# A hybrid mixer with a mixture of experts: the merge gates in three fp32r passes, attention's mask fused with its maximum, memory loaded first

## The chip, the cores and the metric

One core of a Trainium2 chip runs the whole kernel. The metric is the device time of one execution in microseconds (us); the input arrays lie in the chip's memory when it starts. The core's engines are TensorE (PE in the profile; its weight loads PEld), VectorE (DVE), ScalarE (ACT), GpSimd (POOL) and SyncE (SP), whose queue issues the transfers. The kernel before takes 1305.42 us, the median of 3 runs (1305.41 to 1307.28).

## The reference

Input x is 256 tokens of width 1024, fp32. One layer is computed:

```python
h = _layer_norm(x, ln_emb_g, ln_emb_b)
z = h @ w_in                      # split into q, k, v (three kinds), nsa gates, u, qm, g_mrg
y_nsa = _nsa(q, kc, vc, ks, vs, kw, vw, g_nsa, ...) @ w_nsa_out
y = _s5(u, ...)                   # a linear recurrence over the tokens, 32 groups x 64 states
ga, gb = split(gelu(y) @ w_s5_glu); y_s5 = ga * sigmoid(gb)
y_mem = _memory_attention(qm, mem, w_mem_kv) @ w_mem_out
g = sigmoid(g_mrg).reshape(B_, L, N_BRANCH, D_MODEL)
merged = g[:, :, 0] * y_nsa + g[:, :, 1] * y_s5 + g[:, :, 2] * y_mem
h = _layer_norm(ALPHA * h + merged @ w_o, ln1_g, ln1_b)
h = _layer_norm(ALPHA * h + _moe(h, ...), ln2_g, ln2_b)
```

The attention (`_nsa`) has 8 heads of 64 in 2 groups and three branches: over 15 compressed blocks, over selected blocks and over a window. Here all 256 tokens fall into both the selection and the window, each with a causal mask. The memory attention has 4 heads of 128 over 256 memory rows. The merge gates g_mrg are three products of h with a weight of 1024 x 1024 each, one for each branch. The experts are 32, each with weights of 1024 x 2048 and 1024 x 1024; a token goes to four of them.

## The kernel before

The kernel has three stages. The mixer (to some 345 us of the span) computes the layer norm of the input, all projections, the S5 branch, both attentions, the gates and the projection w_o. The router and the second layer norm follow. Then the 32 experts run one after another, and the last layer norm ends the kernel.

All weights come in chunks of 128 x 2048 fp32 (1 MB), each into one slot of four pools of slots (u, w, s, z with 11, 3, 4 and 4 slots). A transfer starts when its slot is free. Weights of the first experts are loaded ahead into slots of these pools as far as they are free. The queue of SyncE issues all these transfers in one fixed order.

The mixer's order of work is a string of steps, ORDER (line 49), which is written out by hand: v and k are memory values and keys, P0 to P7 the pairs of the S5 branch, V, q, r, m projections and rotations, c0 and c1 the two compressions, e0 and e1 the additions to h (the layer norm's scale and bias for the residual), a0 to a3, b0 to b3 and g0 to g3 the gates of the S5, the memory and the attention branch, N0 to N3 pairs of attention heads, h0 to h3 memory heads, s and o output products. Within an engine the framework's scheduler then orders the instructions of these steps, with this string as their priority, and the result is fixed when the program is built: an engine takes its instructions in that order and waits at the first whose data isn't there.

What the change touches:

A gate step (gate_step, line 710, through feature_major, line 230) loads one chunk of w_g, multiplies its 2 x 8 blocks of 128 x 128 with hT (the normalised input, features on partitions, 256 tokens) in fp32, and copies the 128 x 512 result out on ScalarE (line 712). In the profile each fp32 matmul has two records (`L238 ... mm<-hT,w`).

The output products (s, o, N's w_nsa_out, w_o) use another form: split (line 184) rounds a tile to fp32r on ScalarE (L186) and takes the rest by a subtraction on VectorE (L187), split_half (line 189) does so for half a chunk in a slot of pool s (tile hl), and mm3 (line 197) makes three fp32r matmuls (L199, L200, L201) from high and low parts.

An S5 pair (line 449) makes an angle tile on ScalarE (L456), rounds it by adding and subtracting a large number on VectorE (L457), subtracts (L458, in the profile by the helper's line L80) and goes on to sine and cosine, eight products (`v<-sc,z`, `z<-sc,z`), a scan (L485) and more products. The compressions c0 and c1 (line 576) transpose keys or values (L583), add a position vector on VectorE (`xa<-tr,s_pe_k_cmp`, by L80) and multiply (L597).

Attention (nsa_pair, line 659): for each of two token tiles t and two groups g the scores of two heads lie in a PSUM bank; VectorE adds the mask (`pr<-sc,mask`, by L80), takes the negated maximum (L679), ScalarE takes Exp with its sum (L681), VectorE inverts the sum, multiplies by the branch gate (L683, L684, L80) and scales the probabilities (L687), and TensorE transposes them (L696).

The loads at the start are issued in the order x, a small vector, mem, two chunks of w_memk, the first of w_u.

## Time and profile before

| | |
|---|---|
| runs | 1305.42 us median (1305.41 to 1307.28) |
| profiled execution | 1305.18 us, its span 1303.4 us |
| mean granted TensorE clock | 0.984 |
| TensorE busy | 1226.3 us (94%), 7085 records |
| VectorE busy | 578.5 us (44%) |
| ScalarE busy | 245.5 us (19%) |
| moved by the transfers | 451.94 MB, mean 347 GB/s |

The profile shows one execution. A row of a timeline gives when a group of like instructions starts, how long it lasts, its engine, line, operation and tiles, how many there are, and in brackets how long the engine stood idle before it and what ended the wait. Matmuls overlap: of a matmul the time from one start to the next counts, not its own length. A granted clock of 1.00 is 2.4 GHz, one of 0.50 is 1.2 GHz.

### The profile page before, as it was taken

How to read it: one execution, taken by the hardware profiler on the slowest of the kernel's cores; microseconds unless marked ns; L12 is line 12 of the kernel's file. 1: busy time of each engine (PE TensorE's matmuls, PEld its weight loads, DVE VectorE, ACT ScalarE, POOL GpSimd, SP SyncE). 2: the span in 40 equal slices, each digit the busy share in tenths (PEclk: the TensorE clock that was granted, in tenths of full speed). 3: DMA queues.
4: the chain of work that ended last, by engine and by line, in shares of the span. 5: the costliest groups of instructions: out<-in, count | busy, mean ns of one | idle time of the engine just before them, and what ended most of it. 6: DMA issues, size and time to landing. Idle time of an engine off the chain costs nothing. (4 is left out here: it accounts for less than half of the span.)

```text
span 1303.4 us, 17567 instructions
## 1 busy us (share of the span) xinstructions
PE 1226.3 (94%) x7085; PEld 608.4 (47%) x7086; DVE 578.5 (44%) x1337; ACT 245.5 (19%) x493; POOL 72.2 (6%) x138
## 2 busy tenths in 40 slices
PE   6998999999889999999999999999999999999994
PEld 5656887789644444333333334333333333333331
DVE  5598637488663223433333334333333433332225
ACT  4243315574301000110100011010000110100011
POOL 1000000000110000000000001000000100000001
PEclk9999899999889999999999999999999999999998
DMA  7334435445879999999999999999999999999992
GB/s 267 107 125 159 143 117 177 163 162 214 346 313 411 426 426 426 426 426 426 426 427 425 426 427 427 427 425 427 426 426 427 426 426 426 427 426 426 427 425 83
DMA packets 65333, 451.94 MB, mean 347 GB/s; under 512 B 8896, under 2 KB 9056, under 8 KB 11360
## 3 DMA queue, kind: packets, MB, share of 16 engines
q1 hardware_dynamic: 64960, 450.26, 84.1%
q8 instruction: 57, 0.93, 0.3%
q10 hardware_dynamic: 288, 0.52, 0.1%
q14 instruction: 28, 0.23, 0.0%
HBM read 449.70 MB, written 1.05 MB: 346 GB/s over the span
## 5 line engine op out<-in xcount | busy, mean ns | idle before, releaser
L1025 PE MATMUL pg<-w,xT 128*64 128x512 f32 x1024 | 266.0, 597 | 0.0
L1025 PE MATMUL pl<-w,xT 128*64 128x512 f32 x1024 | 262.7, 592 | 0.0
L1061 PE MATMUL py<-w,aT 128*64 128x512 f32 x1024 | 228.7, 599 | 0.0
L1043 DVE TENSOR_SCALAR gc<-pg 128x256 f32<-128x256 f32 x64 | 24.2, 419 | 336.7 <-PE pg L1025 336.7
L1025 PEld LDWEIGHTS pl<-w,xT 128*64 128x64 f32 x1024 | 78.7, 137 | 133.6 <-issue 125.7
L1068 DVE SCALAR_TENSOR_TENSOR ys<-py,gs,ys 128x512 fp32r<-128x512 f32 x64 | 48.0, 751 | 208.7 <-ACT ys L1067 205.3
L1061 PEld LDWEIGHTS py<-w,aT 128*64 128x64 f32 x1024 | 71.0, 137 | 132.5 <-issue 126.4
L1025 PEld LDWEIGHTS pg<-w,xT 128*64 128x64 f32 x1024 | 72.0, 136 | 129.5 <-issue 118.0
L238 PE MATMUL mm<-hT,w 128*128 128x256 f32 x512 | 120.0, 388 | 1.0 <-ACT hT L323 0.7
L1044 ACT ACTIVATE sg<-gc 128x256 f32<-128x256 f32 x64 | 23.1, 408 | 477.1 <-DVE gc L1043 477.1
L80 DVE TENSOR_TENSOR h<-h,pc 128x512 f32<-128x512 f32 x128 | 82.5, 682 | 56.9 <-PE pc L1076 55.2
L238 PEld LDWEIGHTS mm<-hT,w 128*128 128x128 f32 x512 | 96.3, 193 | 19.4 <-issue 4.9
L83 POOL TENSOR_TENSOR xT<-xT,lc 128x256 f32<-128x256 f32 x64 | 44.7, 698 | 785.0 <-PE py L1057 777.6
L1076 PE MATMUL pc<-ys,ohT 128*128 128x512 f32 x256 | 85.5, 435 | 0.9 <-DVE h L80 0.8
L1067 ACT ACTIVATE ys<-py,gs 128x512 fp32r<-128x512 f32 x64 | 44.0, 688 | 193.6 <-PE py L1061 193.6
L1076 PEld LDWEIGHTS pc<-ys,ohT 128*128 128x128 f32 x256 | 40.2, 188 | 65.8 <-issue 35.1
L1003 PE MATMUL xg<-oh,hb 128*128 128x64 bf16 x1280 | 51.6, 195 | 0.9 <-DVE oh L993 0.9
L1003 PEld LDWEIGHTS <-hb 128*128 128x128 bf16 x1280 | 47.9, 99 | 9.3 <-issue 8.2
L1051 ACT ACTIVATE aT<-pt 128x256 f32<-128x256 f32 x64 | 24.6, 384 | 120.1 <-PE pt L1050 120.1
L1003 PE MATMUL xg<-oh,bias 128*128 128x64 bf16 x256 | 46.1, 195 | 0.0
L1057 PE MATMUL py<-bias,sel 128*64 128x512 bf16 x64 | 25.6, 403 | 20.9 <-DVE lin L1047 20.9
L1050 PE MATMUL pt<-ident,gc 128*128 128x128 f32 x128 | 31.9, 330 | 12.7 <-ACT aT L1051 10.0
(387 smaller groups left out, 1288.4 us busy)
## 6 DMA issues: line engine op xcount, KB each, us to landing
w<-in_w_gate_up SPq DMA_DIRECT2D x256, 1024.0 KB, 19.6
w<-in_w_down SPq DMA_DIRECT2D x128, 1024.0 KB, 19.6
w<-in_w_g SPq DMA_DIRECT2D x12, 1024.0 KB, 5.2
w<-in_w_s_glu SPq DMA_DIRECT2D x4, 1024.0 KB, 4.7
w<-in_w_o SPq DMA_DIRECT2D x4, 1024.0 KB, 6.3
w<-in_w_memk SPq DMA_DIRECT2D x2, 1024.0 KB, 10.0
w<-in_w_u SPq DMA_DIRECT2D x2, 1024.0 KB, 8.9
w<-in_w_memv SPq DMA_DIRECT2D x2, 1024.0 KB, 5.2
```

The source lines that it names most:

```text
L80: V.tensor_tensor(o, x, y, op=op)
L83: G.tensor_tensor(o, x, y, op=op)
L238: PE.matmul(p[:, m * T:(m + 1) * T], w4[:, m, k, :], xT[:, k, :], start=k == 0, stop=k == KT - 1)
L1003: PE.matmul(xg[:, k, :], hb[t][b][:, (4 * i + k) * 128:(4 * i + k + 1) * 128], oh[:, t, :], start=n == 0, stop=n == 5)
L1025: PE.matmul(p_[hf * 64:(hf + 1) * 64, :], lhsT, w[:, o + hf * 512:o + (hf + 1) * 512], start=start, stop=stop)
L1050: PE.transpose(pt[:, c * 128:(c + 1) * 128], g2[:, i, :, c % 2], ident)
L1051: S.activation(aT[:, sl], pt[:, sl], AF.Copy)
L1057: PE.matmul(py[0:64, :], sel, bias[:, 2 * DFF + hf * 512:2 * DFF + (hf + 1) * 512], start=True, stop=False)
L1061: PE.matmul(py[j * 64:(j + 1) * 64, :], a4[:, k // 4, k % 4 + j, :], dn(k + j, hf), start=k + j == 1, stop=k == 6)
L1067: S.activation(y2[:, 0], py, AF.Copy, scale=gs)
L1068: V.scalar_tensor_tensor(y2[:, 1], py, gs, y2[:, 0].bitcast(F32), op0=OP.mult, op1=OP.subtract)
L1076: PE.matmul(pc, ohT[:, t * 128:(t + 1) * 128], ys[hf][:, i], start=i == 0, stop=i == 1)
```

## The change

Gates: hT is split once into hTh and hTl, each half of a chunk of w_g is split as for the output products, and 48 fp32r matmuls take the place of 16 in fp32. Order: c0 and c1 come behind a0 and a1 in place of ahead of e1, P7 comes ahead of b0. Attention: mask addition and maximum become one VectorE operation per head (tensor_tensor_reduce, with the maximum as its accumulator), the small operations serve four heads at once, and the scaling of the probabilities goes to ScalarE, in the memory heads too. S5: ScalarE makes the rounding's first half, VectorE the rest in one operation; two operations of the gelu go to ScalarE. Loads: mem and the first chunk of w_memk come ahead of x.

```diff
@@ -46,7 +46,7 @@
 
 NU, NW, NS, NZ = 11, 3, 4, 4
 PATTERN = "uuzzsuuuuwuwwuszssu"
-ORDER = ("v0 P0 v1 k0 P1 k1 P2 V0 P3 V1 q0 q1 r0 e0 r1 P4 P5 m0 c0 m1 c1 e1 a0 a1 P6 a2 a3 b0 b1 P7 "
+ORDER = ("v0 P0 v1 k0 P1 k1 P2 V0 P3 V1 q0 q1 r0 e0 r1 P4 P5 m0 m1 e1 a0 c0 a1 P6 c1 a2 a3 P7 b0 b1 "
          "Y C b2 b3 N0 g0 N1 h0 h1 g1 g2 L1 B g3 N2 h2 s0 s1 h3 L1 L1 N3 s2 s3 o0 o1")
 LOAD1, LOAD2, LOAD3 = 1, 1, 0
 WOT = "uzsssuzu"
@@ -267,10 +267,11 @@
             return emit
 
 
+        mem = load_rows("mem")
+        memk = [chunk(a["w_memk"][0])]
         xin = load_rows("x")
         lec = small("ln_emb_gc", [128, 2, KT])
-        mem = load_rows("mem")
-        memk = [chunk(a["w_memk"][c]) for c in range(2)]
+        memk.append(chunk(a["w_memk"][1]))
         w_u = [chunk(a["w_u"][0])]
         pos_i = small("positions", [128, NT], I32)
         lr = small("s5_a_re", [128, 16])
@@ -444,6 +445,8 @@
 
         half_pi = fp.tile([128, 1], F32)
         G.memset(half_pi, math.pi / 2)
+        magic = fp.tile([128, 1], F32)
+        G.memset(magic, MAGIC)
         ybank = [None]
 
         def s5_pair(jp):
@@ -453,9 +456,10 @@
             cw, sw, w0, w1 = (z4[:, i] for i in range(4))
             vr, vi, ph, sn = (v4[:, i] for i in range(4))
             for jj in range(2):
-                S.activation(ph[:, jj, :], tio, AF.Copy, scale=psh[:, 2 * jp + jj:2 * jp + jj + 1])
-            V.tensor_scalar(sn, ph, MAGIC, MAGIC, op0=OP.add, op1=OP.subtract)
-            tt(ph, sn, ph, OP.subtract)
+                sc_ = psh[:, 2 * jp + jj:2 * jp + jj + 1]
+                S.activation(ph[:, jj, :], tio, AF.Copy, scale=sc_)
+                S.activation(sn[:, jj, :], tio, AF.Identity, scale=sc_, bias=magic)
+            V.scalar_tensor_tensor(ph, sn, MAGIC, ph, op0=OP.subtract, op1=OP.subtract)
             for jj in range(2):
                 j = 2 * jp + jj
                 V.scalar_tensor_tensor(ph[:, jj, :], tio, psl[:, j:j + 1], ph[:, jj, :], op0=OP.mult, op1=OP.add)
@@ -555,7 +559,7 @@
                 S.activation(pm[:, t, :], s3[:, t, :], AF.Exp, bias=mx[:, t:t + 1], accum_out=sums[:, t:t + 1])
             V.reciprocal(sums, sums)
             for t in range(NT):
-                V.tensor_scalar(pm[:, t, :], pm[:, t, :], sums[:, t:t + 1], None, op0=OP.mult)
+                S.activation(pm[:, t, :], pm[:, t, :], AF.Copy, scale=sums[:, t:t + 1])
             p = bank("tr")
             for kk in range(2):
                 for t in range(NT):
@@ -668,23 +672,28 @@
                     PE.matmul(s3, qT[g * 64:(g + 1) * 64, i, t * 128:(t + 1) * 128],
                               kT[g * 64:(g + 1) * 64, :, 0:nk], start=True, stop=True)
                     scs.append(s3)
+
+                mx = f2.tile([128, 4], F32, tag="mx4", name="mx")
+                sums = f2.tile([128, 4], F32, tag="sums4", name="sums")
                 for g in range(2):
-                    hh = 2 * i + g
                     o = 512 * t + g * 2 * nk
-                    pr_ = prs[:, o:o + 2 * nk].rearrange("p (b k) -> p b k", b=2)
-                    pr[g, t] = pr_
-                    mx = f2.tile([128, 2], F32, tag="mx", name="mx")
-                    sums = f2.tile([128, 2], F32, tag="sums", name="sums")
-                    tt(pr_, scs[g], mask[:, None, 256 - nk:256].to_broadcast([128, 2, nk]), OP.add)
-                    V.tensor_reduce(mx, pr_, axis=AX.X, op=OP.max, negate=True)
+                    pr[g, t] = prs[:, o:o + 2 * nk].rearrange("p (b k) -> p b k", b=2)
                     for b in range(2):
-                        S.activation(pr_[:, b, :], pr_[:, b, :], AF.Exp, bias=mx[:, b:b + 1],
-                                     accum_out=sums[:, b:b + 1])
-                    V.tensor_scalar(sums, sums, TINY, None, op0=OP.max)
-                    V.reciprocal(sums, sums)
-                    tt(sums, sums, gn[:, t, hh * 3 + 1:hh * 3 + 3], OP.mult)
+                        V.tensor_tensor_reduce(pr[g, t][:, b], scs[g][:, b], mask[:, 256 - nk:256], 1.0, -3e38,
+                                               op0=OP.add, op1=OP.max, accum_out=mx[:, 2 * g + b:2 * g + b + 1])
+                V.tensor_scalar(mx, mx, -1.0, None, op0=OP.mult)
+                for g in range(2):
                     for b in range(2):
-                        V.tensor_scalar(pr_[:, b, :], pr_[:, b, :], sums[:, b:b + 1], None, op0=OP.mult)
+                        c = slice(2 * g + b, 2 * g + b + 1)
+                        S.activation(pr[g, t][:, b], pr[g, t][:, b], AF.Exp, bias=mx[:, c], accum_out=sums[:, c])
+                V.tensor_scalar(sums, sums, TINY, None, op0=OP.max)
+                V.reciprocal(sums, sums)
+                s4 = sums.rearrange("p (g b) -> p g b", g=2)
+                tt(s4, s4, gn[:, t, :].rearrange("p (h b) -> p h b", b=3)[:, 2 * i:2 * i + 2, 1:3], OP.mult)
+                for g in range(2):
+                    for b in range(2):
+                        c = slice(2 * g + b, 2 * g + b + 1)
+                        S.activation(pr[g, t][:, b], pr[g, t][:, b], AF.Copy, scale=sums[:, c])
             av = bank("av", 1)
             PE.matmul(av[:, :T], cvb[:, i, :], pcT.rearrange("p t c -> p (t c)"), start=True, stop=False,
                       skip_group_check=True)
@@ -707,9 +716,22 @@
             S.activation(qT[:, i, :], av[:, :T], AF.Copy)
 
 
+        hTs = []
+
         def gate_step(b, dst, func=AF.Copy, scale=1.0):
-            return feature_major(lambda c, n: chunk(a["w_g"][4 * b + c], n), hT,
-                                 lambda m, p: S.activation(dst[:, m], p, func, scale=scale))
+            def step(c):
+                if not hTs:
+                    hTs.extend(big("hT" + n, [128, KT, T], F32R) for n in "hl")
+                    split(hTs, hT)
+                w = chunk(a["w_g"][4 * b + c])
+                p = bank()
+                for i in range(2):
+                    w3 = [x.rearrange("p (k c) -> p k c", k=KT) for x in split_half(w, i)]
+                    for k in range(KT):
+                        mm3(p[:, i * T:(i + 1) * T], lambda j: w3[j][:, k, :], lambda j: hTs[j][:, k, :],
+                            k == 0, k == KT - 1)
+                S.activation(dst[:, 2 * c:2 * c + 2], p.rearrange("p (m t) -> p m t", m=2), func, scale=scale)
+            return step
 
         g1_step, g2_step, g0_step = gate_step(1, macc), gate_step(2, th2), gate_step(0, th0, AF.Tanh, 0.5)
 
@@ -1159,8 +1181,8 @@
 def gelu2(nc, dst, x, s):
 
     V, S = nc.vector, nc.scalar
-    V.tensor_tensor(s, x, x, op=OP.mult)
-    V.tensor_scalar(s, s, 0.044715, 1.0, op0=OP.mult, op1=OP.add)
+    S.activation(s, x, AF.Square)
+    S.activation(s, s, AF.Copy, scale=0.044715, bias=1.0)
     V.tensor_tensor(s, s, x, op=OP.mult)
     S.activation(s, s, AF.Tanh, scale=math.sqrt(2.0 / math.pi))
     V.scalar_tensor_tensor(dst, s, 1.0, x, op0=OP.add, op1=OP.mult)
```

On TensorE, where the first gate and the compression c0 stand (gate step a0 is mm_952 before and mm_886 after, a1 after is mm_983; mm_891 is m1; tr_850, xa_859 and tr_942, xa_951 are c0's, tr_909 is c1's). Before:

```order
L238 MATMUL mm_891<-hT_197,w_889 128x256 x10
L583 MATMUL tr_850<-ident_61,qk_391 64x128 x8
L238 MATMUL mm_891<-hT_197,w_889 128x256 x3
L473 MATMUL sc_1005<-uT_229,w_118 128x256 x2
L473 MATMUL sc_1129<-uT_229,w_118 128x256 x2
L597 MATMUL tr_867<-w_865,xa_859 32x128 x16
L602 MATMUL tr_886<-stack_66,hs_884 128x32
L583 MATMUL tr_909<-ident_61,mis_392 64x128 x8
L238 MATMUL mm_952<-hT_197,w_950 128x256 x16
```

After:

```order
L200 MATMUL mm_886<-hTl_881,hl_914 128x256
L201 MATMUL mm_886<-hTh_880,hl_914 128x256
L587 MATMUL tr_942<-ident_61,qk_391 64x128 x8
L199 MATMUL mm_983<-hTh_880,hl_984 128x256
L200 MATMUL mm_983<-hTl_881,hl_984 128x256
L201 MATMUL mm_983<-hTh_880,hl_984 128x256
...
L200 MATMUL mm_983<-hTl_881,hl_1011 128x256
L201 MATMUL mm_983<-hTh_880,hl_1011 128x256
L199 MATMUL mm_983<-hTh_880,hl_1011 128x256
L601 MATMUL tr_959<-w_957,xa_951 32x128 x16
L200 MATMUL mm_983<-hTl_881,hl_1011 128x256
```

Before, between c0's transposes and its product with xa_859 there stand three matmuls of m1 and four S5 products, and a0 comes behind all of c0. Now the transposes stand behind a0, and the product with xa_951 behind most of a1.

On VectorE at the same place (h_173 are the additions to h, v4 and z4 tiles of an S5 pair, hl halves of gate weights). Before:

```order
L457 TENSOR_SCALAR v4_991<-v4_991 128x512
L80 TENSOR_TENSOR h_173<-h_173,lgb_719 128x1024 x2
L80 TENSOR_TENSOR v4_786<-v4_786,z4_785 128x512 x2
L80 TENSOR_TENSOR v4_991<-v4_991 128x512
L80 TENSOR_TENSOR xa_859<-tr_850,s_pe_k_cmp_396 64x16x15 x4
L485 SCALAR_TENSOR_TENSOR v4_786<-z_mag_288,v4_786 128x256 x4
L461 SCALAR_TENSOR_TENSOR v4_991<-tio_284,z_psl_342,v4_991 128x256 x2
L80 TENSOR_TENSOR z4_785<-z4_785,v4_786 128x512 x2
L80 TENSOR_TENSOR v4_786<-z4_785,v4_786 128x512
L80 TENSOR_TENSOR xa_918<-tr_909,s_pe_v_cmp_398 64x16x15 x3
```

After, from the split of hT (hTl_881) on, with the S5 products left out:

```order
L80 TENSOR_TENSOR h_173<-h_173,lgb_725 128x1024 x2
L187 TENSOR_TENSOR hTl_881<-hT_197,hTh_880 128x2048
L80 TENSOR_TENSOR h_173<-h_173,lgb_725 128x1024
...
L80 TENSOR_TENSOR h_173<-h_173,lgb_725 128x1024
L462 SCALAR_TENSOR_TENSOR v4_1040<-v4_1040 128x512
L80 TENSOR_TENSOR v4_793<-v4_793,z4_792 128x512
L187 TENSOR_TENSOR hl_984<-w_981,hl_984 128x1024
L80 TENSOR_TENSOR v4_793<-v4_793,z4_792 128x512
L187 TENSOR_TENSOR hl_1011<-w_981,hl_1011 128x1024
L465 SCALAR_TENSOR_TENSOR v4_1040<-tio_284,z_psl_342,v4_1040 128x256 x2
L489 SCALAR_TENSOR_TENSOR v4_793<-z_mag_288,v4_793 128x256 x4
L80 TENSOR_TENSOR xa_951<-tr_942,s_pe_k_cmp_398 64x16x15 x4
```

The splits of the gates (hl_984 and hl_1011 for a1) now stand among the S5 operations and the additions to h, and c0's xa behind both of a1's.

On VectorE in the first attention pair (pr_1608 the probabilities, mx_1613 and mx_1635 the maxima of two token tiles, csm and pc the compressed branch). After:

```order
L654 TENSOR_SCALAR csm_1483<-csm_1483 128x8
L187 TENSOR_TENSOR hl_1901<-w_1871,hl_1901 128x1024
L682 ISA pr_1608,mx_1635<-sc_1631,mask_375 128x256
L682 ISA mx_1635 128x1
L682 ISA pr_1608,mx_1635<-sc_1631,mask_375 128x256
L682 ISA mx_1635 128x1
L684 TENSOR_SCALAR mx_1613<-mx_1613 128x4
L655 RECIPROCAL csm_1483<-csm_1483 128x8
L80 TENSOR_TENSOR csm_1483<-csm_1483,gn_406 128x8
L80 TENSOR_TENSOR pc_1464<-pc_1464,csm_1483 128x8x15
L187 TENSOR_TENSOR ys_1409<-bcr_111,ys_1409 128x1024
L682 ISA pr_1608,mx_1635<-sc_1633,mask_375 128x256
```

Each fused operation stands there with two rows, and a token tile's maxima are negated in one operation behind its four.

## Rows read from the trace of the kernel before

**Rows 1.** Busy time by stretch: the stretch in us, its length, then for each engine its busy us (and records), the granted TensorE clock, the transfer engines' mean busy share and GB/s.

```profile
97.80:130.30 32.50, 27.84 (x166) 19.53 (x168) 28.02 (x59) 10.51 (x21) 0.00 (x0) 0.96 0.45 159
...
162.90:195.50 32.60, 32.60 (x182) 26.81 (x180) 11.70 (x27) 5.05 (x8) 0.00 (x0) 1.00 0.32 117
195.50:228.00 32.50, 32.50 (x144) 23.12 (x144) 24.47 (x81) 18.02 (x53) 0.00 (x0) 1.00 0.59 176
228.00:260.60 32.60, 32.60 (x177) 25.02 (x176) 13.60 (x18) 18.06 (x30) 2.69 (x2) 1.00 0.45 164
260.60:325.90 65.30, 63.98 (x459) 55.76 (x458) 53.99 (x102) 39.61 (x74) 0.00 (x0) 1.00 0.51 188
...
372.00:1270.00 898.00, 863.81 (x5120) 343.12 (x5118) 302.25 (x677) 92.42 (x191) 51.80 (x91) 1.00 1.01 426
```

The order of the engines is PE, PEld, DVE, ACT, POOL.

**Rows 2.** The same view of 5 us ahead of the experts.

```profile
365.00:370.00 5.00, 5.00 (x56) 3.08 (x55) 4.16 (x12) 0.00 (x0) 1.84 (x3) 0.82 0.01 3
```

**Rows 3.** TensorE's timeline in the gates.

```profile
157.96 23.15 PE L238 MATMUL mm<-hT,w 128*128 128x256 f32 x106
```

**Rows 4.** ScalarE's timeline there: the first and the last of four gate results.

```profile
160.43 0.60 ACT L712 ACTIVATE macc<-mm 128x512 f32<-128x512 f32 x1 [3.94 <-PE mm L238]
...
181.15 0.60 ACT L712 ACTIVATE th<-mm 128x512 f32<-128x512 f32 x1 [6.31 <-PE mm L238]
```

**Rows 5.** TensorE's timeline in the s5 output: the first and the last of 12 fp32r matmuls in a row.

```profile
252.84 0.28 PE L199 MATMUL mm<-ys,hl 128*128 128x256 f32 x1
...
254.15 0.28 PE L201 MATMUL mm<-ys,hl 128*128 128x256 f32 x1
```

**Rows 6.** TensorE's timeline around c0.

```profile
121.19 1.09 PE L583 MATMUL tr<-ident,qk 128*64 128x128 f32 x16
...
129.04 1.94 PE L597 MATMUL tr<-w,xa 128*32 128x128 f32 x32 [4.19 <-DVE xa L80]
131.36 0.63 PE L602 MATMUL tr<-stack,hs 128*128 128x32 f32 x2 [0.39 <-ACT hs L600]
131.92 1.98 PE L583 MATMUL tr<-ident,mis 128*64 128x128 f32 x16
133.83 9.27 PE L238 MATMUL mm<-hT,w 128*128 128x256 f32 x32
```

**Rows 7.** VectorE's timeline: c0's xa, and its next work behind the S5 pairs that ended at 157.9 us.

```profile
127.13 1.65 DVE L80 TENSOR_TENSOR xa<-tr,s_pe_k_cmp 64x240 f32<-64x240 f32 x4
...
182.20 0.42 DVE L80 TENSOR_TENSOR v<-sc,z 128x256 f32<-128x256 f32 x1 [24.27 <-PE sc L473]
```

**Rows 8.** Busy time by stretch again, of 5 us behind c0's stall and of 5 us in the s5 output.

```profile
130.00:135.00 5.00, 4.61 (x41) 3.59 (x34) 4.80 (x11) 2.35 (x5) 0.15 (x1) 0.50 0.58 202
...
260.00:265.00 5.00, 4.13 (x30) 3.40 (x29) 4.91 (x9) 3.83 (x4) 0.00 (x0) 1.00 0.20 26
```

**Rows 9.** TensorE's timeline at the start.

```profile
8.69 3.46 PE L220 MATMUL sc<-ident,mem 128*128 128x128 f32 x16 [8.69 <-DMA mem<-in_mem]
...
21.80 0.70 PE L238 MATMUL mm<-hT,w 128*128 128x256 f32 x2 [0.70 <-ACT hT L323]
```

**Rows 10.** VectorE's timeline at the start: the layer norm's statistics.

```profile
4.47 1.28 DVE L290 BATCH_NORM_STATS2 bs<-x 128x6 f32<-128x512 f32 x2 [1.88 <-DMA x<-in_x]
```

**Rows 11.** SyncE's queue: small loads that wait for transfers before them.

```profile
9.78 0.33 SPq L281 DMA_DIRECT2D bcr<-in_s_c_re  x1
12.25 0.33 SPq L282 DMA_DIRECT2D bcr<-in_s_c_im  x1
```

**Rows 12.** Groups of instructions by form: line, engine, operation, tiles and shapes, count, then busy us, mean ns of one, and idle time before them with its releasers. The splits of half a chunk.

```profile
L187 DVE TENSOR_TENSOR hl<-w,hl 128x1024 fp32r<-128x1024 f32 x24 | 29.0, 1220 | 15.0 <-ACT hl L186 15.0
L186 ACT ACTIVATE hl<-w 128x1024 fp32r<-128x1024 f32 x24 | 24.9, 1054 | 13.7 <-PE mm L201 12.4 <-DMA w<-in_w_o 1.1
```

**Rows 13.** The same view: the angle of an S5 pair and its rounding.

```profile
L456 ACT ACTIVATE v<-tio,z_psh 128x256 f32<-128x256 f32 x16 | 7.2, 499 | 1.2 <-PE av L499 1.2
...
L457 DVE TENSOR_SCALAR v<-v 128x512 f32<-128x512 f32 x8 | 3.6, 456 | 1.3 <-ACT v L456 1.3
```

**Rows 14.** The same view: attention's softmax.

```profile
L681 ACT ACTIVATE pr<-pr,mx 128x256 f32<-128x256 f32 x16 | 8.0, 502 | 3.9 <-DVE sums L80 2.9 <-DVE pr L687 0.9
...
L681 ACT ACTIVATION_READ_ACCUMULATOR pr<-pr,mx 128x1 f32 x32 | 6.1, 190 | 0.0
L80 DVE TENSOR_TENSOR pr<-sc,mask 128x512 f32<-128x512 f32 x8 | 5.5, 684 | 1.0 <-PE sc L668 1.0
L679 DVE TENSOR_REDUCE mx<-pr 128x2 f32<-128x512 f32 x8 | 5.4, 680 | 0.0
...
L687 DVE TENSOR_SCALAR pr<-pr,sums 128x256 f32<-128x256 f32 x16 | 4.9, 348 | 0.1
...
L687 DVE TENSOR_SCALAR pr<-pr,sums 128x128 f32<-128x128 f32 x16 | 3.7, 282 | 0.0
...
L80 DVE TENSOR_TENSOR pr<-sc,mask 128x256 f32<-128x256 f32 x8 | 3.2, 420 | 6.9 <-PE sc L668 6.9
L679 DVE TENSOR_REDUCE mx<-pr 128x2 f32<-128x256 f32 x8 | 3.1, 408 | 0.0
...
L683 DVE TENSOR_SCALAR sums<-sums 128x2 f32<-128x2 f32 x16 | 2.6, 160 | 2.4 <-ACT pr L681 2.4
```

**Rows 15.** TensorE's timeline in the s5 output.

```profile
264.14 0.39 PE L199 MATMUL mm<-ys,hl 128*128 128x256 f32 x1 [0.87 <-ACT e L793]
```

## Prediction

> **What bounds the kernel now.** I read the busy times by stretch first, then the transfers ahead of the experts, then TensorE's timeline up to that point, and last the engines that feed it. By stretch [rows 1] the reader is to see two kernels in one. From 372 to 1270 us the transfers are busy without a gap at 426 GB/s: the expert weights set the time, and nothing in the change touches them. Before, from 163 to 326 us, TensorE is busy in nearly every microsecond at full clock, with transfers between 117 and 188 GB/s: there the order of TensorE's work sets the time. Between the two, in 365 to 370 us, the transfers stand at 3 GB/s [rows 2]: the weight slots are full, and the next transfer waits until the experts begin to use them. In both kernels the transfers behind that point stand in the same order behind the same waits. So a mixer that ends X us sooner starts the saturated stage X us sooner, and the kernel ends X us sooner. I look only for X.
>
> The profiled execution took 1305.18 us (span 1303.4, 1.8 outside of it), 0.24 less than the median of 1305.42. The sum is made against 1305.2.
>
> **The gates on TensorE.** Each of 12 gate steps is 16 fp32 matmuls, shown as 32 records. 106 such records take 23.15 us at 157.96 us, 0.218 each [rows 3]. Of four gate results in that stretch the first leaves at 160.43 and the last at 181.15 us [rows 4]: three intervals of 6.91 us, a step each. The new form needs three fp32r matmuls for each of the 16, so 48. The s5 output already runs in this form: its records go from 252.84 to 254.15 us in 11 steps, 0.119 us each [rows 5]. I take 48 x 0.119 = 5.70 us. The gain is 12 x (6.91 - 5.70) = 14.5 us. It is the upper bound; if each half loses an interval at both its ends to a change of the kind of matmul, a step takes 4 x 0.12 more, and the gain is 12 x 0.73 = 8.8.
>
> **The stall before c0.** TensorE stands 4.19 us, up to 129.04, for xa from VectorE, and 0.39 us more behind it [rows 6]. VectorE wasn't idle: S5 products and four additions to h stood in front of xa in its order, and it took xa up at 127.13 us [rows 7]. The granted clock is 0.50 in the 5 us from 130 on [rows 8], that is the lower level of 1.2 GHz. In it a0's 32 records took 9.27 us instead of 6.91, and 16 transposes at 131.92 us 1.98 us where as many took 1.09 at 121.19 [rows 6]. The stall costs 4.6 + 2.4 + 0.9 = 7.9 us. The change puts a0 ahead of c0, so that the xa additions have a gate step to hide behind: -7.9, between 0 (another wait with the same effect) and -7.9.
>
> **Memory first.** TensorE begins at 8.69 us, when mem lands behind x [rows 9]; x is there at 4.47 us [rows 10]. With mem in front TensorE could start 4.2 us sooner. The second megabyte is then memk's first chunk, which lands about when mem does now, so its projection of 32 records (7.0 us by the pitch) can begin near 10. But x lands third. The queue's small loads wait on the transfers one after another, until 9.78 (second half of mem) and 12.25 us (memk's first chunk) [rows 11]; so x lands around 12, 7 us or so later than now, and the layer norm with its transposes and hT, which now gives its first matmul at 21.80 us [rows 9], has less slack than that. I take -2, between -4.2 (all of the earlier start) and +2 (hT later by more than is gained in front).
>
> **What is new on VectorE and ScalarE.** Each half of a gate weight needs a ScalarE rounding of 1054 ns and a VectorE difference of 1220 ns [rows 12], so a step takes 2.4 us of VectorE and, with a result's copy of 0.6 [rows 4], 2.7 us of ScalarE, of 5.7. Once, hT is split (128x2048, by twice the rows 2.4 and 2.1 us). From 163 to 195 us VectorE is busy 11.7 of 32.6 us [rows 1], and it stands idle 24.27 us before 182.20 [rows 7], so the late gates are covered. The early ones aren't: from 97.8 to 130.3 us VectorE is busy 28.02 of 32.5. I walked along its new order with the old durations. From the end of hT's split to the end of a1's first half there stand 1.2 (addition to h) + 2.7 (eight S5 products) + 1.2 (h) + 1.2 (two more S5 operations) + 1.2 (the half itself) = 7.5 us, against TensorE's 5.7 for a0 and 0.6 for eight transposes: a wait of 1.2. Then 0.6 + 1.2 + 0.9 + 2.4 (scan) + 1.65 (xa) = 6.8 us to c0's xa, against 2.9 for a1's first half and some 2 of its second: a wait of 1.9. Carried on alike (S5 products, a scan, c1's xa between the splits of a2 and a3) this gives 3 more. I take +6 in all. The lower bound is 0 (VectorE comes early, since memory first and the S5 edits move its work forward), the upper +15 (each of six early steps waits 2.5 us, as long as one scan or two additions to h). What is queued behind a split that waits for ScalarE is the S5 chain, and TensorE's products of P6 and P7 wait for that.
>
> The other edits of S5: one operation of VectorE in place of two (L457, 456 ns [rows 13], and a subtraction over 128x512, about 0.68 as other additions of that size) saves some 0.4 us in each of eight pairs, and ScalarE gets two activations more of 499 ns. Two operations of the gelu go to ScalarE. TensorE is busy beside all of it. I cost it at nothing on its own; it is part of VectorE's coming early, and if that cover is gone, eight pairs bring 3 us either way.
>
> **Attention.** Mask and maximum cost VectorE 5.5 + 5.4 + 3.2 + 3.1 us, three kinds of small operations up to 2.6 each, and the scaling 4.9 + 3.7: some 33 us [rows 14]. The 64 fused operations aren't in the trace. As an addition alone, 128x512 in 684 and 128x256 in 420 ns, 128x256 is 0.42 and 128x128 by the step between them 0.29: 64 x 0.355 = 23 us. With a second part like ScalarE's accumulator read, 190 ns, they take 35. With 5 us of small operations, now half as many, VectorE has 28 to 40 us instead of 33: a gain of 5 to a loss of 7 on an engine that isn't the bound there. The scaling goes to ScalarE at up to 502 ns, the time of its Exp: 16 us at most instead of 8.6, on an engine that is busy 36 of 65 us from 195.5 to 260.6 [rows 1]. What can reach TensorE is the longer chain of a head pair: maximum, Exp of both groups, sums, scaling, transposes. Its cover is gate work, and the six gate steps in this stage give 6 x 1.21 = 7.3 us less of it. Bounds: -1.3 (the only idle time there now, 65.3 - 63.98) to +7.3 (all that those gates save is waited away). I take +3, nearest to single waits like the 0.87 us before 264.14 [rows 15], once in each of four pairs.
>
> Two rules of the Trainium skill speak against this part. By "VectorE: DVE Perf Modes", section "The perf-mode tier table", an fp32 operation of a tensor with a scalar in SBUF runs at double rate and a reduction at single rate. The rows agree: the scaling of 256 elements takes 348 ns, the reduction of as many 408, of 512 680. So the change takes from VectorE what it does cheaply, and ScalarE pays more; by that rule it brings nothing, and the sum stays. By the same page, section "Two Vector instructions with no wait between them", an operation that writes out its accumulator is two instructions. No row here shows one on VectorE; by it the dearer end, 40 us, would hold.
>
> **Sum.** -14.5 - 7.9 - 2 + 6 + 3 = -15.4 us: 1305.2 - 15.4 = 1289.8, or 1290 for a median.
>
> **Rivals.**
> *More gain:* VectorE comes early, attention hides, memory gives 4: -14.5 - 7.9 - 4 = -26, some 1279. For it: 24 us of idle VectorE before 182 us. Against: the walk above. 1276 to 1283; chance 0.10.
> *VectorE becomes the bound of the early gates,* and attention waits: +15 and +7.3 instead of +6 and +3 leave -2, some 1303; half of the step there 1296. For it: 28.02 of 32.5 us busy. Against: the S5 pairs run out after 157 us, and half the gate steps come later. 1296 to 1302.6; chance 0.16.
> *The experts begin no sooner,* since transfers or the router set their start: 1305. For it: the stage before them holds work that no gate touches. Against: 3 GB/s in 365 to 370 us. Chance 0.05, for this or for any cancelling.
> *Slower: the clock.* If the short waits on splits bring TensorE to the lower level, as the one before 129 us did, gates run at half speed, 5.7 us more for each. With all six early ones that is +34: 1305.2 - 15.4 + 34 = 1324; it decides from three steps on (17 us eat the gain). For it: 0.50 behind a stall of 4 us. Against: from 260 to 265 us TensorE is busy 4.13 of 5 us, and the clock stays at 1.00 [rows 8]. Chance 0.07.
>
> **Numbers.** My forecast, 1283 to 1296 as its own range, has 0.62. The range is 1280 to 1302: of the first rival 0.07 lies below, and 0.13 of the other cases above. A measurement of this kernel can tell 0.2%, 2.6 us, from no change. Faster: 0.62 + 0.10 + 0.16 = 0.88; same 0.05; slower 0.07.
>
> **What would show it.** Right: gate records 0.119 us apart; no wait of over 2 us before c0's transposes, and a clock of 1.00 from 120 to 160 us; three or more waits of 1 to 2 us on hl or xa between a1 and a3; the saturated stage beginning 15 us sooner at the same 426 GB/s. Wrong: a pitch well over 0.12; waits of TensorE on hl of over 2.5 us in each early step; a granted clock of 0.5 among the gates; TensorE idle for over 10 us between 190 and 300 us behind ScalarE's scaling or the fused operations; or a first matmul on hT after 22 us.

## The result

The changed kernel takes 1287.61 us (median of 4 runs, 1285.96 to 1289.27), the kernel before 1306.35 us in the same comparison: a ratio of 0.9861, 95% interval 0.9848 to 0.9873. That is 18.2 us less by the ratio. The forecast was 1290, and its direction held. The profiled execution took 1288.12 us (span 1286.4), 17.1 less than the profiled one before; the forecast's sum was 15.4. Behind this near agreement two terms were too good and one too bad, by several microseconds each, so the closeness is in part luck.

Busy time by stretch, after (columns as in [rows 1]):

```profile
100.00:120.00 20.00, 18.76 (x100) 13.65 (x99) 19.82 (x36) 12.69 (x21) 0.00 (x0) 1.00 0.51 177
120.00:140.00 20.00, 19.61 (x170) 17.59 (x169) 19.93 (x35) 9.84 (x16) 0.16 (x1) 0.98 0.53 190
140.00:160.00 20.00, 20.00 (x177) 16.98 (x177) 17.64 (x32) 9.89 (x19) 0.00 (x0) 0.93 0.57 206
...
240.00:260.00 20.00, 18.18 (x115) 13.82 (x114) 11.37 (x36) 19.88 (x53) 0.00 (x0) 1.00 0.29 106
```

VectorE is busy 39.75 of 40 us from 100 to 140, and yet TensorE stands idle only 1.6 us there. From 240 to 260 us ScalarE is full. The start and the first gate step on TensorE's timeline (the start answers to [rows 9], the rows of L587 and L601 to [rows 6]):

```profile
4.60 3.64 PE L220 MATMUL sc<-ident,mem 128*128 128x128 f32 x16 [4.60 <-DMA mem<-in_mem]
9.28 8.95 PE L238 MATMUL mm<-memT,w 128*128 128x256 f32 x32 [1.04 <-DMA w<-in_w_memk]
18.07 1.04 PE L319 MATMUL tr<-ident,h 128*128 128x128 f32 x8
19.43 0.70 PE L238 MATMUL mm<-hT,w 128*128 128x256 f32 x2 [0.33 <-ACT hT L324]
...
23.97 11.49 PE L238 MATMUL mm<-hT,w 128*128 128x256 f32 x52 [0.81 <-DVE hT L326]
...
121.55 0.47 PE L199 MATMUL mm<-hTh,hl 128*128 128x256 f32 x1
...
127.58 1.09 PE L587 MATMUL tr<-ident,qk 128*64 128x128 f32 x16
128.60 0.39 PE L199 MATMUL mm<-hTh,hl 128*128 128x256 f32 x1
...
134.05 1.08 PE L601 MATMUL tr<-w,xa 128*32 128x128 f32 x32 [0.39 <-issue]
```

The first gate step, a0, lasts from 121.55 to 127.58 us, a1 begins at 128.60, and the 4.19 us in front of c0's product have become 0.39. VectorE's rows for the split of hT and for the first halves of a1's and of b2's weight:

```profile
117.97 2.29 DVE L187 TENSOR_TENSOR hTl<-hT,hTh 128x2048 fp32r<-128x2048 f32 x1
...
126.29 1.23 DVE L187 TENSOR_TENSOR hl<-w,hl 128x1024 fp32r<-128x1024 f32 x1
...
170.00 1.23 DVE L187 TENSOR_TENSOR hl<-w,hl 128x1024 fp32r<-128x1024 f32 x1 [1.23 <-ACT hl L186]
```

The largest waits of TensorE up to 360 us, whom it waited for, total, times and longest:

```profile
PE sc L220 <- DMA mem<-in_mem: 4.6, 1, 4.6
PE mm L953 <- DVE selb L949: 3.6, 1, 3.6
PE mm L931 <- DVE xT L226: 1.9, 2, 1.6
PE mm L199 <- ACT e L815: 1.7, 1, 1.7
PE mm L238 <- DMA w<-in_w_memk: 1.0, 1, 1.0
```

None is a wait on a split of a gate weight (the second and third belong to the router, the fourth to the s5 output). The end of the mixer is read from its last product with w_o, before and then after:

```profile
342.52 0.39 PE L201 MATMUL av<-hl,mgTl 128*128 128x512 f32 x1
```

```profile
324.73 0.39 PE L201 MATMUL av<-hl,mgTl 128*128 128x512 f32 x1
```

That is 17.8 us sooner; 17.0 arrive at the end of the span. To see where they come from, I added up, over all rows of TensorE's timeline, the time from each row's start to the next, less idle time:

| what TensorE does | before, us | after, us | difference |
|---|---|---|---|
| gates and the other products with hT | 116.6 | 28.2 + 74.9 (gates) | -13.5 |
| c0 and c1: waits and products with xa | 7.9 | 2.4 | -5.5 |
| S5 products and outputs (sc, av by v) | 17.3 | 20.3 | +3.0 |
| start, to the first products with hT | | | -1.4 |
| waits on qk (rotation), e (s5 output), pcT (compressed attention) | 1.26 | 2.54 | +1.3 |

The start is -4.1 (mem lands), -0.7 (transposes of h and the wait among them), +1.0 (wait for memk), +1.9 (its projection takes longer), +0.1 (waits on hT) and +0.4 (transposes of mem). The rest is -1.6 in many small pieces.

The S5 products take longer at a lower clock. By 4 us, after:

```profile
136.00:140.00 4.00, 4.00 (x20) 2.88 (x19) 4.00 (x6) 2.02 (x5) 0.00 (x0) 0.90 0.70 254
140.00:144.00 4.00, 4.00 (x26) 1.70 (x26) 3.83 (x11) 1.25 (x5) 0.00 (x0) 0.67 0.74 252
180.00:184.00 4.00, 4.00 (x22) 2.97 (x20) 3.81 (x10) 0.09 (x1) 0.00 (x0) 0.57 0.54 223
```

TensorE is busy all of these 12 us, and the clock falls all the same.

Groups by form, after (as [rows 12] and [rows 14]):

```profile
L187 DVE TENSOR_TENSOR hl<-w,hl 128x1024 fp32r<-128x1024 f32 x48 | 58.2, 1222 | 18.1 <-ACT hl L186 17.8
...
L696 ACT ACTIVATE pr<-pr,sums 128x256 f32<-128x256 f32 x16 | 6.9, 506 | 0.7 <-DVE sums L80 0.7
L682 DVE CUSTOM_DVE_ANT_0 pr<-sc,mask 128x256 f32<-128x256 f32 x16 | 6.1, 420 | 1.4 <-PE sc L672 1.3
L696 ACT ACTIVATE pr<-pr,sums 128x128 f32<-128x128 f32 x16 | 5.1, 393 | 0.0
L682 DVE CUSTOM_DVE_ANT_0 pr<-sc,mask 128x128 f32<-128x128 f32 x16 | 3.7, 287 | 5.3 <-PE sc L672 3.5 <-ACT bias L777 1.8
L682 DVE DVE_READ_ACCUMULATOR2_ANT mx<- 128x1 f32 x32 | 2.7, 84 | 0.0
```

### The profile page after: what moved, and what is told of

The parts are those of the page before. It is cut to its first block, busy times and chain, and to the rows that moved or that the text cites. A ratio compares the mean times of both kernels' runs of the same rounds, so it can differ in the third digit from the quotient of the medians.

```text
span 1286.4 us, 18050 instructions
## 1 busy us (share of the span) xinstructions
PE 1216.3 (95%) x7277; PEld 607.8 (47%) x7278; DVE 585.9 (46%) x1326; ACT 294.0 (23%) x580; POOL 72.6 (6%) x139
## 5 line engine op out<-in xcount | busy, mean ns | idle before, releaser
L187 DVE TENSOR_TENSOR hl<-w,hl 128x1024 fp32r<-128x1024 f32 x48 | 58.2, 1222 | 18.1 <-ACT hl L186 17.8
L201 PE MATMUL mm<-hTh,hl 128*128 128x256 f32 x192 | 56.0, 292 | 0.1
L199 PE MATMUL mm<-hTh,hl 128*128 128x256 f32 x192 | 55.8, 291 | 0.0
L200 PE MATMUL mm<-hTl,hl 128*128 128x256 f32 x192 | 55.4, 289 | 0.0
L186 ACT ACTIVATE hl<-w 128x1024 fp32r<-128x1024 f32 x48 | 49.8, 1053 | 17.8 <-PE mm L201 9.6
```

The source lines that it names most:

```text
L186: S.activation(hi, src, AF.Copy)
L187: (eng or V).tensor_tensor(lo, src, hi.bitcast(F32), op=OP.subtract)
L199: PE.matmul(o, lhsT(0), rhs(0), start=start, stop=False)
L200: PE.matmul(o, lhsT(0), rhs(1), start=False, stop=False)
L201: PE.matmul(o, lhsT(1), rhs(0), start=False, stop=stop)
```

## The experiments

Times stand beside the kernel before in the same comparison; with the changed kernel (ratio 0.9861) they are compared by ratio, and each ratio is good to some 0.0016, 2 us. Of each kernel one execution is profiled.

**Gates back in fp32.**

```diff
-            def step(c):
-                if not hTs:
-                    hTs.extend(big("hT" + n, [128, KT, T], F32R) for n in "hl")
-                    split(hTs, hT)
...
-            return step
+            return feature_major(lambda c, n: chunk(a["w_g"][4 * b + c], n), hT,
+                                 lambda m, p: S.activation(dst[:, m], p, func, scale=scale))
```

> The changed kernel with its gate steps back in fp32 (no splits of gate weights or of hT), everything else kept. Theory A (TensorE's own time decides: by the account of its rows the gates with their switches gave 11.8 us): 11 to 13 us over the changed kernel, some 1299.5 us. Theory B (VectorE decides how much of that arrives, so without the splits the waits behind them go too): less than 8 us over it, below 1296 us.

Measured: 1300.51 us, ratio 0.9954 (0.9937 to 0.997), 12 us over the changed kernel. Theory A holds: the gates are worth about what TensorE's rows say (11.1, see below), and no waits on splits stand against it. Not all of the 12 need be the matmuls' own: in this trace TensorE also waits 2.1 us for a gate's weights and 2.6 on e.

**The gates alone,** the reverse experiment.

```diff
-            return feature_major(lambda c, n: chunk(a["w_g"][4 * b + c], n), hT,
-                                 lambda m, p: S.activation(dst[:, m], p, func, scale=scale))
+            def step(c):
+                if not hTs:
+                    hTs.extend(big("hT" + n, [128, KT, T], F32R) for n in "hl")
+                    split(hTs, hT)
...
+            return step
```

> The kernel before with the new gate steps alone. Theory A (TensorE's own time decides): 11 to 13 us under the kernel before, 1293.5 to 1295.5 us. Theory B (without the lighter S5 and attention work and the new order VectorE is late with the splits): less than 7 us under it, 1299 us or more, with waits of TensorE on hl among the first gate steps.

Measured: 1294.98 us, ratio 0.9923 (0.9906 to 0.994), 10.8 us under the kernel before by medians and 10.1 by the ratio: just short of A's numbers and far from B's. The waits of TensorE there from 110 to 200 us:

```profile
PE sc L473 <- DVE z L80: 1.6, 1, 1.6
PE tr L597 <- ACT hl L186: 1.4, 1, 1.4
PE av L499 <- DVE v L80: 0.5, 1, 0.5
```

None is a wait on VectorE's part of a split (the second stands before c0's product, which starts just after xa is there, at 128.75 us). So the gates don't need the lighter S5 and attention work, nor the new order.

**The old order of steps in the changed kernel.**

```diff
-ORDER = ("v0 P0 v1 k0 P1 k1 P2 V0 P3 V1 q0 q1 r0 e0 r1 P4 P5 m0 m1 e1 a0 c0 a1 P6 c1 a2 a3 P7 b0 b1 "
+ORDER = ("v0 P0 v1 k0 P1 k1 P2 V0 P3 V1 q0 q1 r0 e0 r1 P4 P5 m0 c0 m1 c1 e1 a0 a1 P6 a2 a3 b0 b1 P7 "
```

> The changed kernel with the old order of steps (c0 and c1 ahead of the gates, P7 late). Theory A (the stall before c0 and the low clock behind it cost 7.9 us, of which the new order gave 3 back by slow S5 products): about 5 us over the changed kernel, some 1292.5 us, with a wait on xa of some 4 us and a granted clock of 0.5 behind it. Theory B (splits now stand ahead of xa on VectorE and lengthen that wait): 8 us or more over it, 1296 us or more.

Measured: 1298.0 us, ratio 0.9935 (0.9919 to 0.9952), 9.7 us over the changed kernel. That is B's number, but not by B's reason: the wait on xa is 3.59 us, shorter than before the change, and 0.83 us more behind it make some 4 us. The rest is the clock, which stands at 0.50 behind that wait, as Theory A said, and once more later. By 4 us, in this kernel:

```profile
180.00:184.00 4.00, 4.00 (x39) 3.91 (x38) 4.00 (x7) 1.48 (x2) 0.00 (x0) 0.84 0.64 254
184.00:188.00 4.00, 4.00 (x19) 3.96 (x19) 3.85 (x11) 0.09 (x1) 0.00 (x0) 0.50 0.02 4
188.00:192.00 4.00, 4.00 (x18) 2.83 (x16) 1.10 (x5) 0.22 (x1) 0.00 (x0) 0.50 0.00 0
192.00:196.00 4.00, 4.00 (x18) 2.85 (x17) 0.48 (x1) 1.74 (x3) 0.00 (x0) 0.50 0.00 0
```

In these 16 us the clock loses 6.6 us (4 x (0.16 + 3 x 0.50)), in the changed kernel's row of 180 to 184 us 1.7; TensorE is busy throughout.

**The new order alone,** on the kernel before (the same lines, the other way).

> The kernel before with the new order of steps alone. Theory A: the wait of 4.6 us before c0 and its low clock go, 5 to 8 us under the kernel before, 1298.5 to 1301.5 us. Rival (the wait moves to another place, or S5 products run slow elsewhere): within 2 us of the kernel before.

Measured: 1297.86 us, ratio 0.9939 (0.9923 to 0.9956), 8.0 us under the kernel before. Theory A: the order, P7's new place included, is worth the 7.9 us that the prediction gave the stall and its clock. Together with the gates alone that is 18 to 19 us, the whole of the change; taken out of the changed kernel one by one, gates, order and loads are worth 12, 9.7 and 4, more than the whole. So the parts don't simply add up.

**The loads in their old order.**

```diff
-        mem = load_rows("mem")
-        memk = [chunk(a["w_memk"][0])]
         xin = load_rows("x")
         lec = small("ln_emb_gc", [128, 2, KT])
-        memk.append(chunk(a["w_memk"][1]))
+        mem = load_rows("mem")
+        memk = [chunk(a["w_memk"][c]) for c in range(2)]
```

> The changed kernel with the loads in their old order (x, the small vector, mem, both chunks of w_memk). Theory A (the first matmul on hT came 2.4 us sooner, of which waits behind it took 1): 1 to 2.5 us over the changed kernel, 1289 to 1290 us. Theory B (the early start is hidden): no difference, within 0.7 us.

Measured: 1292.31 us, ratio 0.9894 (0.9877 to 0.991), some 4 us over the changed kernel, more than A gave it. Its start explains 1.8: a0 begins at 123.35 us in place of 121.55.

```profile
22.15 0.70 PE L238 MATMUL mm<-hT,w 128*128 128x256 f32 x2 [0.71 <-ACT hT L323]
...
123.35 0.47 PE L199 MATMUL mm<-hTh,hl 128*128 128x256 f32 x1
```

Its mixer ends 3.2 us later than the changed kernel's. The clock keeps 1.00 around 140 us here, but the rows show longer stretches at a lower clock between 176 and 188 and from 248 to 256 us; why these change with the loads, or whether they do because of them, stays open.

**The old attention.** The mask, maximum and scaling are put back on VectorE, with before's lines of nsa_pair and mem_head. (The file of this run also repeats the definitions around nsa_pair, of which the later ones count, and so has one small tile twice.)

```diff
-                        V.tensor_tensor_reduce(pr[g, t][:, b], scs[g][:, b], mask[:, 256 - nk:256], 1.0, -3e38,
-                                               op0=OP.add, op1=OP.max, accum_out=mx[:, 2 * g + b:2 * g + b + 1])
...
+                    tt(pr_, scs[g], mask[:, None, 256 - nk:256].to_broadcast([128, 2, nk]), OP.add)
+                    V.tensor_reduce(mx, pr_, axis=AX.X, op=OP.max, negate=True)
```

> The changed kernel with the old mask, maximum and scaling on VectorE, in the attention pairs and the memory heads. Theory A (attention's engines hide behind TensorE either way): within 1.5 us of the changed kernel. Theory B (VectorE's 20 us more, beside the splits, reach TensorE): 4 us or more over it, with waits of TensorE between 200 and 270 us. A third reading (the scaling on ScalarE lengthens the chain of a head pair): faster than the changed kernel by 1 to 2 us.

Measured: 1288.96 us, ratio 0.9865 (0.9848 to 0.9881): no difference, theory A.

**The old rounding and gelu.** The gelu's first two lines go back to VectorE too.

```diff
-                S.activation(sn[:, jj, :], tio, AF.Identity, scale=sc_, bias=magic)
-            V.scalar_tensor_tensor(ph, sn, MAGIC, ph, op0=OP.subtract, op1=OP.subtract)
...
+            V.tensor_scalar(sn, ph, MAGIC, MAGIC, op0=OP.add, op1=OP.subtract)
+            tt(ph, sn, ph, OP.subtract)
```

> The changed kernel with the old rounding of the S5 pairs and the old gelu on VectorE. Theory A (TensorE hides it): within 1 us of the changed kernel. Theory B (VectorE is the bound around the first gate steps, so eight times 0.4 us ahead of them arrive): 2 to 4 us over it.

Measured: 1287.76 us, ratio 0.9867 (0.985 to 0.9883): no difference, theory A.

**Every gate split's subtraction twice.**

```diff
-                    w3 = [x.rearrange("p (k c) -> p k c", k=KT) for x in split_half(w, i)]
+                    parts = split_half(w, i)
+                    V.tensor_tensor(parts[1], w[:, i * 1024:(i + 1) * 1024], parts[0].bitcast(F32), op=OP.subtract)
+                    w3 = [x.rearrange("p (k c) -> p k c", k=KT) for x in parts]
```

> The changed kernel with every gate split's subtraction on VectorE made twice: 24 operations of 1.2 us more, 12 of them in the first six steps; the output is unchanged. Theory A (VectorE has slack of more than that, my walk overstated the waits): under 3 us over the changed kernel. Theory B (VectorE is about co-bound in the first gate steps, as it is busy 59.4 of 60 us from 100 to 160 us nearly): 8 us or more over it, most of it as waits on hl between 120 and 165 us.

Measured: 1307.11 us, ratio 1.0004 (0.9992 to 1.0016), 19 us over the changed kernel: Theory B's size. (VectorE's busy time from 100 to 160 us is 57.4 us in the rows of the changed kernel, not the 59.4 of the expectation.) TensorE, in this kernel:

```profile
134.57 0.58 PE L201 MATMUL mm<-hTh,hl 128*128 128x256 f32 x1 [5.04 <-DVE hl L730]
147.66 1.86 PE L601 MATMUL tr<-w,xa 128*32 128x128 f32 x32 [1.59 <-DVE xa L80]
```

and VectorE in front of the first of these:

```profile
129.05 1.22 DVE L187 TENSOR_TENSOR hl<-w,hl 128x1024 fp32r<-128x1024 f32 x1
130.19 0.87 DVE L465 SCALAR_TENSOR_TENSOR v<-tio,z_psl,v 128x256 f32<-128x256 f32 x2
130.98 2.43 DVE L489 TENSOR_TENSOR_SCAN v<-z_mag,v 128x256 f32<-128x256 f32 x4
133.32 1.20 DVE L730 TENSOR_TENSOR hl<-w,hl 128x1024 fp32r<-128x1024 f32 x1
```

The second half's split has an S5 scan in its middle, and TensorE waits 5 us for it, then runs at 0.50 of its clock. But the waits on hl are 5.9 us in all, not most of the 19. Other waits, of up to 3.2 us on a gate's result (th, at 217 us), and stretches at the lower clock make up the rest: by 2 us, the mixer loses 11.9 us to the clock here, and 3.4 in the changed kernel. So in the changed kernel the splits come in time, but with little to spare; how little is read from its own rows below, for here the second subtraction didn't only add its 1.2 us but came behind the scan.

**Scaling back on VectorE, the fused operation kept.**

```diff
-                        S.activation(pr[g, t][:, b], pr[g, t][:, b], AF.Copy, scale=sums[:, c])
+                        V.tensor_scalar(pr[g, t][:, b], pr[g, t][:, b], sums[:, c], None, op0=OP.mult)
```

The memory heads' line changes in the same way.

> The changed kernel with the fused mask and maximum kept, and the scaling of the probabilities back on VectorE (attention pairs and memory heads). Theory A (ScalarE is full from 240 to 260 us, 19.88 of 20, and TensorE waits 1.68 us there for its result of the s5 output): 1 to 2 us under the changed kernel, and that wait gone. Rival (VectorE's 11 us more come among its splits): 1 to 3 us over it. Neither: within 0.7 us.

Measured: 1285.22 us, ratio 0.9839 (0.9826 to 0.9853), the lowest of all. It is 2.4 us under the changed kernel by medians and 2.9 by ratios, but the intervals overlap. The wait of 1.68 us on e is gone, and one of 1.29 us on the scaled probabilities has come in its place. So the place of TensorE's wait there moves with the scaling; how much the move back brings isn't settled within 2 us.

**c1 behind a2,** `P6 a2 c1 a3` in place of `P6 c1 a2 a3`.

> The changed kernel with c1 behind a2 in place of behind P6, which takes c1's transposes and P6's outputs apart on TensorE. Theory A (these small matmuls in one place bring the clock to 0.5 at 139 to 143 us, without a wait, for about 2 us): 1 to 2.5 us under the changed kernel, and a clock of 1.00 from 120 to 160 us. Rival (VectorE has no slack there, c1's xa then delays a3's splits): 0 to 3 us over it.

Measured: 1290.04 us, ratio 0.9887 (0.9871 to 0.9904), 2.4 us over the changed kernel by medians and 3.4 by the ratio, but its runs go from 1286.89 to 1293.35 us, and the two intervals just meet; the profiled execution is the shortest, 1.2 us under the changed kernel's. Its rows by 4 us:

```profile
136.00:140.00 4.00, 3.97 (x32) 2.92 (x30) 3.49 (x6) 1.14 (x2) 0.00 (x0) 1.00 0.79 274
140.00:144.00 4.00, 4.00 (x40) 3.85 (x40) 3.85 (x10) 3.54 (x8) 0.00 (x0) 1.00 0.60 250
180.00:184.00 4.00, 4.00 (x19) 3.11 (x17) 3.26 (x12) 0.30 (x1) 0.00 (x0) 0.50 0.54 227
184.00:188.00 4.00, 4.00 (x24) 2.87 (x20) 0.87 (x2) 2.12 (x2) 0.00 (x0) 0.78 0.00 0
```

With c1 and P6 apart the clock stays at 1.00 up to 144 us. That doesn't show theory A, for the run with the loads in their old order and the one with the old rounding have c1 and P6 together and keep 1.00 there too. The lower stretch behind the compressed scores is longer, and no time is seen to be won.

**Both of these.**

> The changed kernel with both: scaling on VectorE and c1 behind a2. If both theories A hold: 2 to 4 us under the changed kernel, below 1286 us; if the rivals hold: 1 us or more over it.

Measured: 1288.34 us, ratio 0.9858 (0.9839 to 0.9878): neither reading, no difference from the changed kernel.

## Why the prediction was right, and where it wasn't

**What bounds the kernel** was right. The mixer ended 17.8 us sooner and the profiled kernel 17.0 to 17.1.

**The gates,** 14.5 forecast, 11.1 in the account (13.5 less the 2.4 of a0's low clock, which the prediction booked with the stall), 12 by the experiment, 10 to 11 alone. The mechanism was right; the term was mis-sized in "48 x 0.119 = 5.70 us". The first step took 6.03 us (121.55 to 127.58), and the 12 together 74.9, 6.24 each: the switches to other matmuls, priced only in the lower bound, and stretches at a lower clock belong to it.

**The stall before c0,** 7.9 forecast: the new order alone gives 8.0. In the changed kernel 5.5 of wait and slow products and the 2.4 of a0 do go, but S5 products and outputs give 3.0 back at a clock that falls without a wait. The sign that should have shown the step right, "a clock of 1.00 from 120 to 160 us", failed, and one of those for wrong, "a granted clock of 0.5 among the gates", came.

**Memory first,** 2 forecast, 1.4 in the account; the experiment says 4, and 1.8 of that is seen at the start. So the size was right. Of the 4.1 us that mem lands sooner, 1.0 goes to the wait for memk and 1.9 to its projection, which starts at the lower clock (see the end).

**New waits on VectorE's splits,** +6 forecast. This is the step that failed: no wait on a split is among the rows (the sign "three or more waits of 1 to 2 us on hl or xa" failed), and the wait on xa is 0.39 us where the walk gave 1.9 at this place and 6 in all. VectorE's work had the length that the walk gave it (from the end of hT's split at 120.2 us to the end of a1's first half at 127.4 it is 7.2 us, 7.5 by the walk), but TensorE wasn't at a0 when the split ended: it came at 121.55, 1.4 us later, needed 6.03 for it and 1.02 for the transposes, which the walk had at 5.7 and 0.6. So it came to a1 at 128.60, 1.1 us behind the end of the split, in place of a wait of 1.2. The walk had started both engines at the same moment. That the margin is thin was right: the first half of a1 is ready 1.1 us ahead, that of a2 as long ahead of the first matmul that needs its low part. The tightest is b2's, behind a late rounding on ScalarE: it ends at 171.23 us, just ahead of its matmul, and TensorE idles 0.1 us. Doubling the subtraction costs 19 us. The bound of 0 named as reason that VectorE comes early through memory first and the S5 edits. Undoing the S5 edits changes nothing, and with the loads in their old order both engines come 1.8 us later and the 1.1 us stay, so that reason falls.

**Attention,** +3 forecast, +0.8 in waits, and nothing by the experiment. The count was wrong: there are 32 fused operations, not 64 (four pairs, two token tiles, two groups, two heads), and the accumulator read is 84 ns, not 190; so VectorE's share fell to 6.1 + 3.7 + 2.7 = 12.5 us and the small operations, below the 28 to 40 given. It did not reach TensorE. By the Trainium skill, "VectorE: DVE Perf Modes", section "Two Vector instructions with no wait between them", an operation that also writes out its accumulator is two instructions; the trace agrees, with the row of 84 ns beside 420 and 287. By the Trainium skill, the same page, section "The perf-mode tier table", `tensor_scalar` on fp32 in SBUF runs at double rate and `tensor_reduce` at single. The trace agrees: 128 elements more cost the scaling 66 ns, 256 more the maximum 272 [rows 14]. So VectorE was the cheap place for the scaling: on ScalarE it takes 506 ns where VectorE took 348 [rows 14]. The run with the scaling put back leans the same way, within its noise.

**The rivals.** VectorE did not become the bound; with the subtractions made twice TensorE does wait for it, 5.9 us on hl. The clock did fall, as the slower rival had it, but for a few microseconds and not behind waits on splits. Against the sum of -15.4 the account reads: gates 3.4, clock 3.0 and start 0.6 us of gain too much; splits 6 and attention some 2 us of loss too much. Errors of 7 and 8 us cancel, and that the sum came out near is luck in this respect.

## What to carry to other kernels

Before pricing a new wait by walking an engine's queue, fix the moment at which the other engine arrives: a late start of 1.4 us and a step that took longer than priced took away a wait of 1.2, and all those that were derived from it. Measure slack, by the time from the end of a split to the matmul that needs it or by doubling the suspected cost: no wait in a trace doesn't mean that there is room. And when faster matmuls take the place of slow ones, price a step by its whole time between other work, not by the distance of two records in the middle of it.

## What the runs showed of the hardware

The granted clock fell to 0.5 with TensorE busy in every microsecond. In the changed kernel by 1 us:

```profile
138.00:139.00 1.00, 1.00 (x6) 0.63 (x5) 1.00 (x3) 0.15 (x1) 0.00 (x0) 1.00 0.94 385
139.00:140.00 1.00, 1.00 (x7) 0.94 (x7) 1.00 (x2) 0.97 (x2) 0.00 (x0) 0.62 0.24 98
140.00:141.00 1.00, 1.00 (x6) 0.25 (x5) 0.97 (x3) 0.23 (x2) 0.00 (x0) 0.50 0.52 82
```

In front of the falls stand matmuls that fill little of the array: 32 rows (`sc<-uT,w 32*128`) ahead of 139 us, 16 rows (`tr<-cv,wide 16*128`) and 15 columns (`sc<-ckT,qq`) ahead of 180 us. But the kernel before has the same stretch of them, and its clock stays at 1.00. Before:

```profile
187.48 1.99 PE L623 MATMUL tr<-cv,wide 16*128 16x64 f32 x16
189.40 1.74 PE L636 MATMUL sc<-ckT,qq 64*128 64x15 f32 x22
```

```profile
188.00:192.00 4.00, 4.00 (x42) 3.41 (x40) 3.74 (x10) 0.72 (x2) 0.00 (x0) 1.00 0.02 4
```

In the changed kernel and ten of the eleven runs the clock falls somewhere between 175 and 197 us, in different lengths; in the kernel before and in the one with its gates back in fp32 it doesn't. So the small matmuls alone don't explain the fall; what does stays open, and no run took them away.

At the start both kernels run at the lower level, which the lengths of the records show and the view by stretch does not: the trace's record of the clock begins only at 11.82 us before and at 12.94 after, and the view counts what lies ahead as 1.00. Before, the transposes of mem stand 0.21 us apart up to 11.70 us and 0.11 behind. After, the memory projection's records are up to 766 ns long, from 12.8 us on 379; so its 32 records take 8.95 us in place of 7.07. TensorE starts 4.1 us sooner, but the clock rises 1.1 us later. In the run with every subtraction made twice, which starts at 4.8 us, the record begins at 7.85; what sets the moment stays open.
